# Attention and output projection of a hybrid trunk layer by seven block products (Strassen's scheme, Winograd's form) in place of eight

## The chip, the cores and the metric

One core of one Trainium2 chip runs the whole program. The metric is the device time of one execution in microseconds; the median of three runs of the kernel before is 1764.46 us (1763.48 to 1765.0).

## What is computed

One streaming step of one layer, for 1024 prompt tokens and 8 times 16 sample tokens (NT = 1152 tokens together), with D_MODEL 1024. The reference, cut to what matters here:

```python
def trunk_layer(...):
    h = rms_norm(x, norm_g) * (1 + scale) + shift
    q, k, v, z_att, z_ssd, xbc, dt_raw, gates = jnp.split(h @ w_in, IN_SPLITS, axis=-1)
    ...
    att_branch = (o_att.reshape(b, s, ATT_WIDTH) * jax.nn.silu(z_att)) @ w_att_proj   # 1024 x 1024
    ...
    y = rms_norm(y per group, ssd_norm_g)                                             # y = scan * silu(z_ssd)
    ssd_branch = y @ w_ssd_proj                                                       # 2048 x 1024
    merged = jax.nn.sigmoid(g_att) * att_branch + jax.nn.sigmoid(g_ssd) * ssd_branch
    out = x + gate * (merged @ w_out)                                                 # 1024 x 1024
```

All data are float32. The change concerns two of the three products above: the one with `w_att_proj` and the one with `w_out`.

## The kernel before

Activations lie channel-major: 128 channels on the partitions, 1152 tokens along the free axis. A projection of 1024 channels reads 8 such operand blocks and makes 8 output blocks.

**A product.** A float32 product is made of three float16 products: each operand is split into a high half (ScalarE casts it with a scale, L627 for weights, L1946 for activations) and a low half (VectorE: value times scale minus high half, L628 and L1948), and TensorE adds high·high, high·low and low·high (L709, L710, L712) into one PSUM tile. `dense` (from L694) makes an output tile of 128 channels by 384 tokens with 8 steps over the operand blocks (4 in the SSD projection), three matmuls each; three tiles make an output block. Tiles called d, g and s come from three PSUM pools of 3, 3 and 1 slots (an s slot has two banks). The first output block of the att and of the output projection (`wide`) and the last one of a product (`last`) make their three tiles side by side, step by step.

**The tail of the program**, with which the change deals. The att projection runs first (`att_dense`, 8 jobs of one output block). Its operands are loaded from DRAM by `att_prep` (SyncE, L1961) and split by `split` (L1943 to L1953); its result is multiplied into the gate block, which `gate_loads` fetched (SyncE, L1969; the evict is L1998, VectorE reading PSUM). Next come four groups of the SSD projection (`ssd_dense(g)`, 4 jobs with two output blocks each, tiles of 12 matmuls): VectorE multiplies a tile with its gate (L2007, reads PSUM) and adds it to the att result (L2008, reads SBUF only). In group 3 each output block is then complete, and `split` makes it an operand of the output projection. Last is `out_dense`, 8 output blocks: VectorE adds gate times tile to x (L2070; the sample columns by L2074 and L2076), and SyncE stores the block (L2081 for the last block, tile by tile, L2083 for the others). Weights of 128×1024 float32 come from DRAM ahead of their use and are split by `w_split`; ScalarE also sums the squares of every weight and operand (`level`, L619). `verdict` (L2047 to L2060) compares these sums with bounds and writes `again`; at the end of the program every engine reads `again` (L3822) and would otherwise run a general kernel, which does not happen here.

**What sets the order.** The program is written as generators that emit work in the order of the dense products, with helper generators beside them (`urgent`, `pause`). A list scheduler, class `Order`, then fixes one order of instructions for each engine from a table of costs. Each engine runs its own list in order. Semaphores between the engines see to the data, so that an instruction that waits holds up all that stands behind it on its engine. GpSimd (Pool) has a mask multiplication of the SSD scan (L1816), small steps of the group norm, and the DMA issues of the stores of gates (L1659) and of y (L1892); it does nothing from the att projection's second half on.

Of the kernel before, what the change touches and what calls it, by code (L numbers as in the profile page):

```python
# [16 lines left out]
P = 128  # L17
# [47 lines left out]
X_MEAN = (0.25, 2.0 ** 19)  # L65

# [353 lines left out]
def trunk_kernel(ctx: ExitStack, tc: tile.TileContext, h, again):  # L420
# [42 lines left out]
    NPART, NOPER = 121, 48  # L463
    sums = fix(NPART + 2 + NOPER)
# [34 lines left out]
    L_TAIL = arena.set_layout(Z0, [("T", 15, NT)])  # L499
    L_SM = arena.set_layout(Z0 + 15 * NT, [("e", 2, 384)])  # L500
# [14 lines left out]
    def alloc(lay, tag, cols):  # L515
        if lay is L_H or lay is L_W or lay is L_W3 or lay is L_Q or lay is L_V:
# [84 lines left out]
    def job(*raw):  # L601
        jobs.append([len(parts) + i for i in range(len(raw))])
        parts.extend(raw)
# [9 lines left out]
    meant = {"w": 0, "x": NPART + 2}  # L613
# [15 lines left out]

    def w_split(i, keep=lambda x: x):  # L630

        n = len(jobs[i])
# [44 lines left out]
    def w_done(i):  # L677
        for x in wsplit.pop(i)[:2]:
            x.free()
# [1255 lines left out]
    gates = []  # L1935

# [16 lines left out]

    att_ops, out_ops = [], []
    ssd_ops = [[] for _ in range(NG)]

    def att_prep():
        yield from ready(lambda: ssd_all[NPAIR])
        for u in range(NU):
            t = yield from walloc(L_TAIL, "T", NT)  # L1960
            dma(t.ap, att_d[u])  # L1961
            yield from pause(3000)
            urgent.append(split(t, att_ops, SA))

    def gate_loads():
        yield from ready(lambda: len(att_ops) >= NU - 1)
        for i in range(16):
            t = yield from walloc(L_TAIL, "T", NT)
            dma(t.ap, gate_d[i])  # L1969
            gates.append(t)  # L1970
            yield from pause(5000 if i < 2 else 10500)

    def ssd_prep(g):
        yield from ready(lambda: len(ssd_ops[g - 1]) == PPG if g else len(att_ops) == NU)
# [16 lines left out]
    def att_dense():  # L1991
        for c in range(8):
            def ev(o, g, tok, ps, c=c):
                while len(gates) <= c:
# [5 lines left out]
            yield from dense(att_ops, ev, last=c == 7, wide=c == 0, other=True)  # L2000

    def ssd_dense(g):
        for cp in range(4):
            def ev(o, g_, tok, ps, cp=cp):
# [42 lines left out]
    def verdict():  # L2047
        w, n = NPART + 2, NPART + 2 + NOPER
        assert meant == {"w": NPART, "x": n}
        nc.scalar.activation(sums[:, NPART:w], par["qk_g"], AF.Square, scale=4.0)  # L2050
        good = alloc(L_TAIL, "T", NT).ap
        ps = pg(NOPER)
        nc.tensor.matmul(ps, ones, sums[:, w:n], start=True, stop=True)
        for a, b, x, (least, most) in ((0, w, sums[:, :w], W_MEAN), (w, n, ps, (P * X_MEAN[0], X_MEAN[1]))):
            nc.vector.tensor_scalar(good[:, a:b], x, least, None, ALU.is_ge)
            nc.vector.scalar_tensor_tensor(good[:, a:b], sums[:, a:b], most, good[:, a:b], ALU.is_le, ALU.mult)
        nc.vector.tensor_reduce(good[:, n:n + 1], good[:, :n], mybir.AxisListType.X, ALU.min)
# [4 lines left out]
    def out_dense():  # L2062
        for c in range(8):
            x = yield from walloc(L_TAIL, "T", NT)
            dma(x.ap, h["xT"][c])

            def ev(o, g, tok, ps, c=c, x=x):
                n = G3 if g < 2 else NP - 2 * G3
                a = g * G3
                nc.vector.scalar_tensor_tensor(x.ap[:, a:a + n], ps[:, :n], m3[:, 16 + c, 0:1], x.ap[:, a:a + n], ALU.mult, ALU.add)  # L2070
                if g == 2:
                    t = alloc(L_SM, "e", P)
                    t3 = t.ap.rearrange("p (b s) -> p b s", s=NS)
                    nc.vector.tensor_tensor(t3, ps[:, n:].rearrange("p (b s) -> p b s", s=NS),  # L2074
                                            m3[:, 16 + c, 1:].unsqueeze(2).to_broadcast([P, NB, NS]), ALU.mult)
                    nc.vector.tensor_tensor(x.ap[:, NP:], x.ap[:, NP:], t.ap, ALU.add)  # L2076
                    t.free()
                if c == 7:
                    if g == 2:
                        verdict()  # L2080
                    dma(h["out_y"][c][:, tok], x.ap[:, tok])  # L2081
                elif g == 2:
                    dma(h["out_y"][c], x.ap)  # L2083
                    x.free()

            yield from dense(out_ops, ev, wide=c == 0, order=(2, 0, 1) if c == 7 else (0, 1, 2))
# [1880 lines left out]
```

## Time and profile before

The profiled execution took 1765.52 us, of which 1763.6 us are the span that the profile covers. The engines in that span:

| engine | busy us | share of the span |
|---|---|---|
| TensorE matmul (PE) | 1738.2 | 99% |
| TensorE weight load (PEld) | 1092.9 | 62% |
| VectorE (DVE) | 1230.0 | 70% |
| ScalarE (ACT) | 957.8 | 54% |
| GpSimd (POOL) | 347.3 | 20% |

The tail by the stretches of the trace (start of the first to start of the next product's first matmul):

| stretch | from us | to us |
|---|---|---|
| att projection | 1376.8 | 1476.0 |
| SSD projection, 4 groups | 1476.0 | 1663.2 |
| output projection | 1663.2 | 1757.3 |
| after the last matmul | 1757.3 | 1763.6 |

How to read it: an engine's busy time is the time in which an instruction of it runs, register, branch and DMA-issuing instructions left out. A row of the timeline gives an instruction's start, its duration, engine, line, operation, what it writes and reads, and in brackets the idle time before it with what ended it. Since successive matmuls overlap, the price of one is the distance from start to start, and not its duration.

### The profile page before, as it was taken

The numbers are of one execution on the slowest core, as the hardware profiler recorded it, in microseconds if no ns is written. First come the engines' busy times: TensorE is split into PE (matmuls) and PEld (weight loads), VectorE is DVE, ScalarE is ACT, GpSimd is POOL, SyncE is SP. The second block draws the span as 40 slices with busy tenths as digits, with TensorE's granted clock in tenths as the row PEclk, the third lists the DMA queues.
The fourth block names the chain that finished last, engine by engine and source line by source line (L and its number), as shares of the span: only waits on it lengthen the run. The fifth ranks groups of instructions, "written<-read, shape, count | busy, mean of one in ns | idle before, by whom it ended". The sixth has DMA issues, their size and how long they took to land.

```text
span 1763.6 us, 34941 instructions
## 1 busy us (share of the span) xinstructions
PE 1738.2 (99%) x13821; PEld 1092.9 (62%) x13821; DVE 1230.0 (70%) x2327; ACT 957.8 (54%) x1903; POOL 347.3 (20%) x624
## 2 busy tenths in 40 slices
PE   7999999999999999999999999999999999999998
PEld 3556556555556566666666666666666556666665
DVE  6458677877776967787878677777775526876732
ACT  8766555556465565656764656456552616342510
POOL 0233323323133011321312131112222100000000
PEclk9999999999999999999999999999999999999999
DMA  9248878988887584533554445435577734311321
GB/s 381 74 125 206 196 213 198 206 211 195 204 232 165 148 230 131 174 114 124 174 158 114 107 132 181 140 117 133 165 227 271 270 103 156 102 49 50 128 104 56
DMA packets 266565, 284.87 MB, mean 162 GB/s; under 512 B 199628, under 2 KB 200664, under 8 KB 266392
## 3 DMA queue, kind: packets, MB, share of 16 engines
q1 hardware_dynamic: 257432, 253.90, 51.9%
q0 software_dynamic: 8960, 28.65, 4.3%
q8 instruction: 110, 1.80, 0.4%
q14 instruction: 63, 0.52, 0.1%
HBM read 192.70 MB, written 43.66 MB: 134 GB/s over the span
## 4 chain that ended last, share of the span: by engine, by line
PE 87%; DVE 5%; ACT 4%; DMA 2%; issue 1%; POOL 1%; SPq 0%; DVEq 0%; POOLq 0%; ACTq 0%
PE d L709 19%; PE d L710 18%; PE d L712 18%; PE d L762 5%; PE d L764 5%; PE d L763 5%; PE g L1368 2%; PE s L1855 2%; PE g L1827 2%; PE g L1875 1%; PE s L1415 1%; PE g L1415 1%; PE g L712 1%; PE g L710 1%; PE g L709 1%
## 5 line engine op out<-in xcount | busy, mean ns | idle before, releaser
L709 PE MATMUL d<-arena 128*128 128x384 f16 x2172 | 709.6, 327 | 1.4 <-ACT arena L1543 1.4
L710 PE MATMUL d<-arena 128*128 128x384 f16 x2172 | 708.7, 326 | 0.0
L712 PE MATMUL d<-arena 128*128 128x384 f16 x2172 | 708.6, 326 | 0.0
L709 PEld LDWEIGHTS <-arena 128*128 128x128 f16 x2280 | 223.5, 98 | 147.8 <-issue 10.5
L712 PEld LDWEIGHTS <-arena 128*128 128x128 f16 x2280 | 223.2, 98 | 147.8 <-issue 0.5
L710 PEld LDWEIGHTS <-arena 128*128 128x128 f16 x2280 | 223.3, 98 | 138.0 <-issue 2.0
L619 ACT ACTIVATE arena<-arena 128x1024 bf16<-128x1024 f32 (+3 forms) x169 | 181.5, 1074 | 145.0 <-DMA arena<-in_wall_dram 82.4
L627 ACT ACTIVATE arena<-arena 128x1024 f16<-128x1024 f32 (+1 forms) x117 | 122.4, 1046 | 124.5 <-PE d L710 112.6
L762 PE MATMUL d<-arena 128*128 128x384 f16 (+1 forms) x568 | 186.8, 329 | 0.0
L764 PE MATMUL d<-arena 128*128 128x384 f16 (+1 forms) x568 | 186.1, 328 | 0.0
L763 PE MATMUL d<-arena 128*128 128x384 f16 (+1 forms) x568 | 186.1, 328 | 0.0
L628 DVE SCALAR_TENSOR_TENSOR arena<-arena 128x1024 f16<-128x1024 f32 (+1 forms) x117 | 145.3, 1246 | 42.3 <-ACT arena L627 41.7
L1308 ACT ACTIVATE arena<-arena 128x640 f32<-128x640 f32 (+4 forms) x144 | 100.8, 701 | 62.6 <-DVE arena L1311 62.1
L1566 DVE SCALAR_TENSOR_TENSOR arena<-arena 128x1176 f32<-128x1176 f32 x72 | 107.2, 1489 | 2.3 <-issue 0.9
L1754 ACT ACTIVATE arena<-arena 128x128 f32<-128x128 f32 x288 | 89.9, 390 | 28.0 <-DMA arena<-acs_d 26.3
L762 PEld LDWEIGHTS <-arena 128*128 128x128 f16 x576 | 56.3, 98 | 50.7 <-issue 17.5
L1344 DVE SCALAR_TENSOR_TENSOR arena<-arena 128x640 f16<-128x640 f32 (+4 forms) x128 | 86.9, 711 | 0.0
L1236 POOL TENSOR_SCALAR arena<-arena 128x16 f32<-128x16 f32 (+1 forms) x24 | 10.0, 415 | 356.3 <-DVE arena L1209 356.1
L764 PEld LDWEIGHTS <-arena 128*128 128x128 f16 x576 | 56.4, 98 | 38.4 <-issue 0.2
L1203 ACT ACTIVATE arena<-d 128x256 f32<-128x256 f32 x71 | 26.8, 378 | 96.1 <-PE d L764 96.1
L763 PEld LDWEIGHTS <-arena 128*128 128x128 f16 x576 | 56.4, 98 | 32.8
L1311 DVE CUSTOM_DVE_ANT_0 arena<-s,arena 128x320 f32<-128x320 f32 (+4 forms) x128 | 60.2, 502 | 19.4 <-PE s L1473 9.4
(242 smaller groups left out, 2596.4 us busy)
## 6 DMA issues: line engine op xcount, KB each, us to landing
arena<-in_wall_dram SPq DMA_DIRECT2D x85, 512.0 KB
arena<-acs_d SPq DMA_DIRECT2D x32, 576.0 KB
arena<-in_kc_dram SPq DMA_DIRECT2D x64, 256.0 KB
arena<-in_vc_dram SPq DMA_DIRECT2D x64, 256.0 KB
arena<-in_wada_dram SPq DMA_DIRECT2D x24, 512.0 KB
arena<-in_xT_dram SPq DMA_DIRECT2D x16, 576.0 KB
gate_d<-arena POOLq DMA_DIRECT2D x48, 192.0 KB, 4.0
arena<-eacs_d SPq DMA_DIRECT2D x32, 288.0 KB
```

Source lines behind the costliest of these rows:

```text
L619: keep(nc.scalar.activation(junk[:, :n], x, AF.Square, scale=scale * n ** -0.5, accum_out=sums[:, c:c + 1]))
L627: keep(nc.scalar.activation(hi, x, AF.Copy, scale=scale))
L628: keep(nc.vector.scalar_tensor_tensor(lo, x, scale, hi, ALU.mult, ALU.subtract))
L709: nc.tensor.matmul(ps, hi.r[:, wc], kh.r[:, tok], start=k == 0, stop=False)
L710: nc.tensor.matmul(ps, hi.r[:, wc], kl.r[:, tok], start=False, stop=False)
L712: nc.tensor.matmul(ps, lo.r[:, wc], kh.r[:, tok], start=False, stop=k == nk - 1)
L762: nc.tensor.matmul(ps, kh.r[:, tok], wh, start=k == 0, stop=False)
L763: nc.tensor.matmul(ps, kh.r[:, tok], wl, start=False, stop=False)
L764: nc.tensor.matmul(ps, kl.r[:, tok], wh, start=False, stop=k == KT - 1)
L1308: nc.scalar.activation(p, p, AF.Exp, bias=sm_[:, 4 + e:5 + e], scale=-1.0, accum_out=sm_[:, 6 + e:7 + e])
L1566: nc.vector.scalar_tensor_tensor(yc, r.ap[:, j:j + n], w4[:, i, j:j + 1], yc, ALU.mult, ALU.add)
L1754: nc.scalar.activation(me[e].ap[:, cs], me[e].ap[:, cs], AF.Relu, scale=-1.0, bias=a4[:, c, hds[e]:hds[e] + 1])
```

## The change

The att and the output projection are done in pairs. Two output blocks c and c+1, the even and odd operand blocks, and the first and second 576 tokens make a 2×2 product of blocks; where eight block products stood, seven are made (q0 to q6), each with 4 steps over pairs of operand blocks. `quad_dense` makes a product as two tiles of 128×288, in the order 0, 1, 5, 6, 4, 3, 2, with the banks taken from the pools s, g and d in turn. What the scheme needs beside the products:

- `quad_split`: four sums of 128×512 weights on Pool for each pair of output blocks; halves of 1024, 1024, 1024 and 512 columns (before: twice 1024).
- `pieces` in place of `split`: for each pair of operand blocks four sums of 128×576 on Pool; halves of 576, 1152, 1152 and 1152 columns (before: twice 1152), and four sums of squares of 576 columns.
- joins: ScalarE copies q0 out of PSUM; six products are joined with a running sum by seven joins of two VectorE additions 128×288 each (one operand in SBUF, one in PSUM; q4 is added into two sums).
- the evicts take 128×576 from SBUF instead of 128×384 from PSUM (att: L2191; out: L2281, and L2284 and L2285 for the samples); the output is stored in 16 parts of 128×576 (L2286).

With these go two more slots of 128×1152 in the tail, loads of gates held back until blocks are used up (`gone`), and a longer `verdict` (emitted with the last pair's product 4). New line numbers: matmuls L776 to L778, joins L790, Pool sums L659 to L662 and L2130 to L2133, halves L635/L636 and L2114/L2116, SSD evicts L2202/L2203, loads of att operands L2151.

```diff
+    def quad_split(i):
...
+        halves(bufs[0].r, bufs[1].r, w[0].ap, SW)
+        nc.gpsimd.tensor_tensor(t[0], b[0], b[1], ALU.add)
+        nc.gpsimd.tensor_tensor(t[1], t[0], a[0], ALU.subtract)
+        nc.gpsimd.tensor_tensor(t[2], a[0], b[0], ALU.subtract)
+        nc.gpsimd.tensor_tensor(t[3], a[1], t[1], ALU.subtract)
...
+        halves(bufs[3].r, bufs[4].r, u[0].ap, SW)
+        halves(k4(bufs[2].r[:, :512]), k4(bufs[2].r[:, 512:]), b[1], SW)
+        halves(bufs[5].r, bufs[6].r, u[1].ap, SW)
...
-    for x in [h["wall"][i] for i in range(29, 85)] + [h["watt"][i] for i in range(8)] + [h["wssd"][i] for i in range(16)] \
-            + [h["wout"][i] for i in range(8)]:
-        job(x)
...
+    for i in range(0, 8, 2):
+        job(h["watt"][i], h["watt"][i + 1], quad=True)
...
+    def quad_dense(ops, evict, last=False):
...
+        def product(q, banks):
+            for k in range(4):
+                while len(ops) <= k:
+                    blocked[0] = "operand"
+                    yield None
+                wh, wl = w(q, k)
+                xh, xl = ops[k][q][:2]
+                for g, ps in enumerate(banks):
+                    c = slice(g * HC, (g + 1) * HC)
+                    nc.tensor.matmul(ps, wh, xh[:, c], start=k == 0, stop=False)
+                    nc.tensor.matmul(ps, wh, xl[:, c], start=False, stop=False)
+                    nc.tensor.matmul(ps, wl, xh[:, c], start=False, stop=k == 3)
+                    yield 3 * 122.0
...
+                nc.vector.tensor_tensor(y.ap[:, c], t.ap[:, c], ps, op)
...
+        b = bank(0)
+        yield from product(0, b)
+        s1 = yield from walloc(L_TAIL, "T", HT)
+        for g, ps in enumerate(b):
+            nc.scalar.activation(s1.ap[:, g * HC:(g + 1) * HC], ps, AF.Copy)
+        b = bank(1)
+        yield from product(1, b)
+        c = yield from joined(s1, b, ALU.add)
+        yield from evict(0, 0, c) or ()
+        b = bank(2)
+        yield from product(5, b)
+        u2 = yield from joined(s1, b, ALU.add)
...
+        b = bank(6)
+        yield from product(2, b)
+        c = yield from joined(u4, b, ALU.add)
+        u4.free()
+        yield from evict(0, 1, c) or ()
+        w_done(i)
...
+    def pieces(ta, tb, ops, scale):
...
+        got[0], = yield from halved(b11, HT)
+        got[1], got[2] = yield from halved(tb.ap[:, :NT], NT)
...
+        nc.gpsimd.tensor_tensor(t1, b12, b11, ALU.subtract)
+        nc.gpsimd.tensor_tensor(t2, b22, t1, ALU.subtract)
+        nc.gpsimd.tensor_tensor(t3, b22, b12, ALU.subtract)
+        nc.gpsimd.tensor_tensor(t4, t2, b21, ALU.subtract)
...
+        got[4], got[5] = yield from halved(u[0].ap[:, :NT], NT)
+        u[0].free()
+        got[6], got[3] = yield from halved(u[1].ap[:, :NT], NT)
...
     def att_dense():
-        for c in range(8):
-            def ev(o, g, tok, ps, c=c):
...
-                x = gates[c].ap[:, tok]
-                nc.vector.scalar_tensor_tensor(x, x, 1.0, ps, ALU.add, ALU.mult)
...
+                x = gates[c + o].ap[:, t * HT:(t + 1) * HT]
+                nc.vector.scalar_tensor_tensor(x, x, 1.0, y.ap, ALU.add, ALU.mult)
...
+            yield from quad_dense(att_ops, ev, last=c == 6)
+            gone[0] = c + 2
...
                 if g == NG - 1 and g_ == 2:
                     gates[8 + c].free()
-                    urgent.append(split(gates[c], out_ops, 0.5 * SM / (SA * SW)))
-
+                    if o:
+                        urgent.append(pieces(gates[c - 1], gates[c], out_ops, 0.5 * SM / (SA * SW)))
...
     def out_dense():
...
+                nc.vector.scalar_tensor_tensor(x.ap[:, a:a + n], y.ap[:, :n], m[:, 0:1], x.ap[:, a:a + n], ALU.mult, ALU.add)
+                if t:
+                    y3 = y.ap[:, n:].rearrange("p (b s) -> p b s", s=NS)
+                    nc.vector.tensor_tensor(y3, y3, m[:, 1:].unsqueeze(2).to_broadcast([P, NB, NS]), ALU.mult)
+                    nc.vector.tensor_tensor(x.ap[:, NP:], x.ap[:, NP:], y.ap[:, n:], ALU.add)
+                dma(h["out_y"][c + o][:, a:a + HT], x.ap[:, a:a + HT])
```

The change also moves instructions on the engines that feed TensorE. Names such as d_17612 are PSUM tiles of the pool d; `arena` is the SBUF.

**VectorE in the last SSD group, before** (L2007 and L2008 are the two evicts of a tile, L1948 a low half of an operand of the output projection, L628 one of a weight):

```order
L1948 SCALAR_TENSOR_TENSOR arena<-arena 128x1152
L2008 TENSOR_TENSOR arena<-arena 128x384
L2007 SCALAR_TENSOR_TENSOR arena<-arena,d_17415 128x384
L2008 TENSOR_TENSOR arena<-arena 128x384
L2007 SCALAR_TENSOR_TENSOR arena<-arena,d_17431 128x384
L2008 TENSOR_TENSOR arena<-arena 128x384
L628 SCALAR_TENSOR_TENSOR arena<-arena 128x1024
L2007 SCALAR_TENSOR_TENSOR arena<-arena,d_17446 128x384
L1948 SCALAR_TENSOR_TENSOR arena<-arena 128x1152
```

VectorE there after the change (L2202 and L2203 are the same evicts, L2116 a low half of an operand or of sums of operands, L636 one of a weight):

```order
L2202 SCALAR_TENSOR_TENSOR arena<-arena,d_17612 128x384
L2116 SCALAR_TENSOR_TENSOR arena<-arena 128x1152
L2203 TENSOR_TENSOR arena<-arena 128x384
L2202 SCALAR_TENSOR_TENSOR arena<-arena,d_17629 128x384
L2116 SCALAR_TENSOR_TENSOR arena<-arena 128x1152
L2203 TENSOR_TENSOR arena<-arena 128x384
L2202 SCALAR_TENSOR_TENSOR arena<-arena,d_17648 128x384
L2116 SCALAR_TENSOR_TENSOR arena<-arena 128x1152
L2203 TENSOR_TENSOR arena<-arena 128x384
L2202 SCALAR_TENSOR_TENSOR arena<-arena,d_17664 128x384
L2116 SCALAR_TENSOR_TENSOR arena<-arena 128x576
```

A low half stands between the two evicts of each tile, four in a row, where before there were one or two in four tiles.

**Pool in the last SSD group, after the change** (the sums of a pair of operands of the output projection and those of its first pair of weights):

```order
L2130 TENSOR_TENSOR arena<-arena 128x576
L2131 TENSOR_TENSOR arena<-arena 128x576
L2132 TENSOR_TENSOR arena<-arena 128x576
L2133 TENSOR_TENSOR arena<-arena 128x576
L659 TENSOR_TENSOR arena<-arena 128x512
L2130 TENSOR_TENSOR arena<-arena 128x576
L660 TENSOR_TENSOR arena<-arena 128x512
L661 TENSOR_TENSOR arena<-arena 128x512
L662 TENSOR_TENSOR arena<-arena 128x512
L2131 TENSOR_TENSOR arena<-arena 128x576
L2132 TENSOR_TENSOR arena<-arena 128x576
L2133 TENSOR_TENSOR arena<-arena 128x576
```

Before, Pool's list holds nothing at this place: its last stores of gates (L1659) stand directly ahead of the end of the program (L3822).

**VectorE at the end of the program, before** (the last tiles of the last output block, d_18289 and d_18316):

```order
L2057 TENSOR_REDUCE arena<-arena 128x1
L2060 TENSOR_SCALAR again<-g_18285 1x1
L2070 SCALAR_TENSOR_TENSOR arena<-d_18289,arena 128x384
L2070 SCALAR_TENSOR_TENSOR arena<-d_18316,arena 128x384
L3822 TENSOR_LOAD again
```

and after it (s_18812 are the two banks of the last product, g_18777 the 1×1 result of the verdict's matmul):

```order
L2264 TENSOR_REDUCE arena<-arena 128x1
L2281 SCALAR_TENSOR_TENSOR arena<-arena 128x576
L790 TENSOR_TENSOR arena<-arena,s_18812 128x288
L2267 TENSOR_SCALAR again<-g_18777 1x1
L790 TENSOR_TENSOR arena<-arena,s_18812 128x288
L2281 SCALAR_TENSOR_TENSOR arena<-arena 128x448
L2284 TENSOR_TENSOR arena<-arena 128x128
L2285 TENSOR_TENSOR arena<-arena 128x128
L4027 TENSOR_LOAD again
```

Behind the last matmul one evict stood on VectorE; now there stand the verdict's write and, behind the join, three more instructions.

More of the change, by code (lines that the diff above doesn't have):

```diff
@@ L65 @@
 X_MEAN = (0.25, 2.0 ** 19)
+H_MEAN = (0.25, 2.0 ** 14)
 class NoSlot(Exception):
@@ L1935, in trunk_kernel @@
     gates = []
+    gone = [0]
     def gates_dense():
@@ L1991, in att_dense, with ev @@
     def att_dense():
[L1992 to L1994 removed]
+        for c in range(0, 8, 2):
+            def ev(o, t, y, c=c):
+                while len(gates) <= c + o:
                     blocked[0] = "gates"
                     yield None
[L1997 to L2000 removed]
+                x = gates[c + o].ap[:, t * HT:(t + 1) * HT]
+                nc.vector.scalar_tensor_tensor(x, x, 1.0, y.ap, ALU.add, ALU.mult)
+                y.free()
+            yield from quad_dense(att_ops, ev, last=c == 6)
+            gone[0] = c + 2
     def ssd_dense(g):
@@ L2062, in out_dense, with ev @@
     def out_dense():
[L2063 to L2086, printed above, removed]
+        for c in range(0, 8, 2):
+            xs = []
+            for o in range(2):
+                x = yield from walloc(L_TAIL, "T", NT)
+                dma(x.ap, h["xT"][c + o])
+                xs.append(x)
+            def ev(o, t, y, c=c, xs=xs):
+                x, n = xs[o], HT if t == 0 else NP - HT
+                a = t * HT
+                m = m3[:, 16 + c + o, :]
+                nc.vector.scalar_tensor_tensor(x.ap[:, a:a + n], y.ap[:, :n], m[:, 0:1], x.ap[:, a:a + n], ALU.mult, ALU.add)
[4 more added lines that the diff above has]
+                dma(h["out_y"][c + o][:, a:a + HT], x.ap[:, a:a + HT])
+                y.free()
+                if c == 6 and (o, t) == (1, 1):
+                    verdict()
+            yield from quad_dense(out_ops, ev)
     def head_dense():
```

174 lines of the change are left out of this document (154 added, 20 removed).

## The prediction

> **What bounds the kernel now.** I read the page first: busy times, the clock and the chain that ended last.
>
> ```profile
> PE 1738.2 (99%) x13821; PEld 1092.9 (62%) x13821; DVE 1230.0 (70%) x2327; ACT 957.8 (54%) x1903; POOL 347.3 (20%) x624
> ...
> PEclk9999999999999999999999999999999999999999
> ...
> PE 87%; DVE 5%; ACT 4%; DMA 2%; issue 1%; POOL 1%; SPq 0%; DVEq 0%; POOLq 0%; ACTq 0%
> ```
>
> TensorE is busy 99% of the span at the full granted clock, and holds 87% of the chain. So the number of matmul columns is the time, as long as the others keep up. Whether they do is read where the change works, in the table by stretch (us, then busy time and count of PE, PEld, DVE, ACT, POOL, then clock, DMA share, GB/s): the att projection, the last SSD group, the output projection.
>
> ```profile
> 1376.80:1476.00 99.20, 99.20 (x627) 58.80 (x625) 39.36 (x53) 37.91 (x57) 3.97 (x10) 1.00 0.48 174
> 1619.40:1666.20 46.80, 46.80 (x290) 28.18 (x288) 35.98 (x58) 22.54 (x29) 0.00 (x0) 1.00 0.34 109
> 1663.20:1757.30 94.10, 94.10 (x581) 56.44 (x579) 32.02 (x61) 21.31 (x31) 0.00 (x0) 1.00 0.27 97
> ```
>
> In both projections that change, VectorE is busy for 40% and 34% of the time: room for more. In the last SSD group it is busy 36.0 of 46.8 us already: there is the narrow place. Pool is idle in all of these but for the start of the att projection.
>
> **The matmuls.** First and last of a stretch of 18 matmuls with 384 columns, and of 15 with 416 (start, duration):
>
> ```profile
> 1749.11 0.33 PE L709 MATMUL d<-arena 128*128 128x384 f16 x1
> ...
> 1751.87 0.33 PE L712 MATMUL d<-arena 128*128 128x384 f16 x1
> 544.77 0.34 PE L762 MATMUL d<-arena 128*128 128x416 f16 x1
> ...
> 547.24 0.34 PE L764 MATMUL d<-arena 128*128 128x416 f16 x1
> ```
>
> From start to start that is 2.76/17 = 0.1624 us at 384 columns and 2.47/14 = 0.1764 at 416. In proportion to the columns 288 take 0.1218 us; along the line through both, 0.1201. Before, each projection has 8 blocks × 3 tiles × 8 steps × 3 = 576 matmuls, 1152 in both: 187.1 us. After, 4 pairs × 7 products × 4 steps × 2 tiles × 3 = 672 each, 1344: 163.7 us (161.4 by the line). The gain is **−23.4 us**, bounds −22 (a row's rounding) and −25.7.
>
> What could hold that up is the weight load, which does not shrink:
>
> ```profile
> L709 PEld LDWEIGHTS <-arena 128*128 128x128 f16 x901 | 88.4, 98 | 59.6 <-issue 2.3
> ```
>
> A load takes 98 ns and runs beside the matmul before it; 122 ns still cover it, so I add nothing. On this the Trainium skill, "TensorE: Matmul & The Clock Gate", section "Back-to-back issue gap", speaks against the change: a stream of pairs of load and matmul is given as some 81 ns at 128 columns and 131 at 512. By an estimate between those figures 384 columns would take 114 ns and 288 take 102, and 1344 × 102 against 1152 × 114 would lose some 6 us. The trace differs, with 162.4 ns at 384 columns, and the rows decide.
>
> **The end.** Now one evict stands behind the last matmul:
>
> ```profile
> 1757.34 0.62 DVE L2070 SCALAR_TENSOR_TENSOR arena<-d,arena 128x384 f32<-128x384 f32 x1 [3.28 <-PE d L712]
> ```
>
> After, the order has join, write of `again` (which waits for a 1×1 matmul behind the last product), join, 448 columns, and two of 128. Durations by these rows:
>
> ```profile
> L2074 DVE TENSOR_TENSOR arena<-d,arena 128x128 f32<-128x128 f32 x7 | 2.0, 280 | 0.0
> L1909 DVE TENSOR_TENSOR arena<-arena,g 128x512 f32<-128x512 f32 x4 | 2.7, 680 | 1.2 <-PE g L1900 1.2
> ```
>
> That is 0.28 us at 128 columns and 0.68 at 512, so some 0.45 for a join, 0.61 for 448. The first join begins before the last matmuls end; 0.2 + 0.45 + 0.61 + 0.28 + 0.28 and half of a join make 2.0, against 0.62: +1.4, and +0.1 for a store of 576 columns in place of 384. **+1.5 us** (0.7 to 2.5).
>
> **Pool and VectorE hold each other up.** The change gives Pool 64 sums: 32 of 512 columns and 32 of 576. By size, from the rows of another Pool addition:
>
> ```profile
> L1240 POOL TENSOR_TENSOR arena<-arena 128x1024 f32<-128x1024 f32 x16 | 30.8, 1925 | 0.1
> L1240 POOL TENSOR_TENSOR arena<-arena 128x256 f32<-128x256 f32 x8 | 5.0, 627 | 0.2
> ```
>
> 1.06 us and 1.17 us, 71 us in all, on an engine that is idle there. They are not free for VectorE:
>
> ```profile
> 1323.93 1.22 DVE L628 SCALAR_TENSOR_TENSOR arena<-arena 128x1024 f16<-128x1024 f32 x1 [3.29 <-ACT arena L627]
> 1354.77 1.64 DVE L628 SCALAR_TENSOR_TENSOR arena<-arena 128x1024 f16<-128x1024 f32 x1
> 1354.56 2.31 POOL L1816 TENSOR_TENSOR rarena<-rarena,arena 128x256 fp32r<-128x256 f32 x2 [1.41 <-PE g L1900]
> 1376.35 0.20 POOL L590 TENSOR_TENSOR arena<-arena 128x9 f32<-128x9 f32 x1
> 1377.48 1.23 POOL L590 TENSOR_TENSOR arena<-arena 128x9 f32<-128x9 f32 x1
> 1377.30 1.36 DVE L1948 SCALAR_TENSOR_TENSOR arena<-arena 128x1152 f16<-128x1152 f32 x1 [0.84 <-ACT arena L1946]
> ```
>
> The same VectorE instruction took 1.22 us alone and 1.64 beside a Pool instruction that began 0.21 us before it; a Pool instruction took 0.20 alone and 1.23, when a VectorE one had begun 0.18 before it, and ended 0.05 after that one. Both sides read two operands from SBUF: one waits for the other. A Pool sum can thus cost VectorE up to its own 1.1 us.
>
> **The last SSD group.** VectorE's pace there, start to start, in before:
>
> ```profile
> 1641.02 1.22 DVE L628 SCALAR_TENSOR_TENSOR arena<-arena 128x1024 f16<-128x1024 f32 x1
> 1642.16 0.55 DVE L2007 SCALAR_TENSOR_TENSOR arena<-arena,d 128x384 f32<-128x384 f32 x1
> 1642.62 1.35 DVE L1948 SCALAR_TENSOR_TENSOR arena<-arena 128x1152 f16<-128x1152 f32 x1
> 1643.89 0.55 DVE L2008 TENSOR_TENSOR arena<-arena 128x384 f32<-128x384 f32 x1
> 1644.36 0.55 DVE L2007 SCALAR_TENSOR_TENSOR arena<-arena,d 128x384 f32<-128x384 f32 x1
> 1644.94 0.56 DVE L2008 TENSOR_TENSOR arena<-arena 128x384 f32<-128x384 f32 x1
> ```
>
> A half of 1024 columns takes 1.14, of 1152 1.27, a tile's two evicts 0.47 + 0.58 = 1.05. (0.60 and 0.69 for 512 and 576, by the columns.) A tile of 12 matmuls takes TensorE 1.949 us. In the order of after, the 14 tiles 8 to 21 of 24 have beside their evicts six halves of 1152, two of 576, four of 1024 and one of 512: 14.7 + 7.6 + 1.4 + 4.6 + 0.6 = 28.9 us on VectorE against 27.3 on TensorE, 1.6 late. With the same stretch come some 14 Pool sums. One delays VectorE by nothing in a gap, by 0.5 where an evict from PSUM stands next (which the lock doesn't hold), by 1.1 before one from SBUF. VectorE has few gaps here, so I take 0.7: 9.8. Three d tiles let VectorE fall behind by two tiles less its own evict, 2 × 1.949 − 0.75 = 3.1. The stall of TensorE is 1.6 + 9.8 − 3.1 = **+8 us** (0 to 14).
>
> **The start of the att projection.** Operands come late here already:
>
> ```profile
> 1376.82 0.33 PE L709 MATMUL g<-arena 128*128 128x384 f16 x1
> 1383.87 1.36 DVE L1948 SCALAR_TENSOR_TENSOR arena<-arena 128x1152 f16<-128x1152 f32 x1 [0.31 <-ACT arena L1946]
> 1370.37 0.34 SPq L1141 DMA_DIRECT2D arena<-ya  x1
> 1374.15 0.20 POOL L1142 TENSOR_SCALAR arena<-arena 128x9 f32<-128x9 f32 x1 [8.34 <-DMA arena<-ya]
> ```
>
> The last operand is split by 1385.2, 8.4 us after the first matmul, and `wide` covers it with 7/8 of 72 matmuls of 0.1624, 10.2 us. After, the order has 75 matmuls, 9.1 us, before the last step of product 5, which needs the fourth pair's sums. On Pool these stand behind gate stores and the norm's small steps that wait for `ya` until 1374.1; four of 1.17 with waits, then a cast and a half of some 1.3 each, give 1384 to 1387 where 1385.9 is needed. Three sums are also ahead of the SSD mask (L1816, done 1356.87; its matmul began 1359.23, quoted next), 3.4 us in a gap of 2.4.
>
> ```profile
> 1359.23 0.77 PE L1900 MATMUL g<-rarena 128*128 128x256 f32 x4
> ```
>
> Together **+3 us** (0 to 9).
>
> **Inside the products.** A pair takes TensorE 168 × 0.1218 = 20.5 us. VectorE has 14 joins (6.3), four evicts (some 3.0), weight halves (4.0): some 13 us, and with four sums at 1.1 under 18. It fits on average; banks of joins that wait behind a half cost something: **+1.75** over eight pairs (0 to 5). Output stores and loads of x move as many bytes as before, in a stretch whose DMA share is 0.27: nothing.
>
> **The sum**: −23.4 + 1.5 + 8 + 3 + 1.75 = −9.1 us. The profiled execution took 1765.52, its span 1763.6 and 1.9 around it; that gives 1756.4. It stood 1.1 above the median of the runs, 1764.46, so I predict **1755 us**.
>
> **Rivals.**
> - *Hidden.* Pool sums fall into gaps of VectorE and the operands arrive in time. For it: Pool's 71 us are spread over some 380 us of tail, and ScalarE's waits leave gaps in VectorE (row L1948 at 1377.30 waited 0.84 for ScalarE). Against it: 28.9 us in 27.3. It gives 1764.5 − 23.4 + 1.5 = 1742.6.
> - *Slower: the lock at full price.* Each critical Pool sum delays the low half or evict behind it by its whole length, and each low half delays the sum that the next half needs. 14 × 1.1 in the last group and two fourth pairs (att and out) with 4 sums of 1.17 that wait 1.25 each, 2.4 × 8 = 19, and 1.6, less 3.1 for the three d tiles and less 2 us in hand at each of the two starts: 29 us; −23.4 + 29 + 1.5 = +7: 1772. It decides from 22 us of such waits, where the gain is gone, some 20 sums at full price. Against it: a Pool sum waits for one VectorE instruction at most, and evicts from PSUM pass. The Trainium skill, "SBUF — State Buffer", section "SBUF: two separate sides", has the pair of ports as a lock held for the whole instruction; by that each collision pays in full, as the rows above bear out, but not how many collide.
> - *The change doesn't do what it says*: matmuls keep 0.1624 at 288 columns, held by the loads. 1344 × 0.1624 = 218.3, +31: 1797. Against it: 98 ns of a load, and 0.1764 against 0.1624 at 416 columns.
>
> **How the numbers follow.** A measurement of this kernel can tell about 0.2%, 3.5 us, from no change: faster is under 1761, slower over 1768. My forecast (1748 to 1761) has 0.52, hidden (1742 to 1748) 0.24, stalls that eat most of the gain (1761 to 1768) 0.09, the lock at full price 0.12, no shrinking 0.03. Faster 0.76, same 0.09, slower 0.15. The range 1742 to 1767 leaves out 0.15 above and a little of hidden below; the unknown terms at their bounds (0 to 28 us of stall) span 1740 to 1772, whose ends need all of them at once.
>
> **What would show it.** Matmuls at L776 with 0.122 us from start to start; if 0.14 or more, the first step is wrong. TensorE idle in the last SSD group, before d tiles that L2202 frees: 8 us; under 3 shows the sums in gaps, over 12 the full price. L2203, L636 and L2116 longer than 0.55, 1.22 and 1.35 beside L659 to L662 and L2130 to L2133. TensorE idle before g and d tiles of products 5 and 6 near the att projection's start: 3. From the last matmul to the end of the span 7.8 in place of 6.3. What would prove me wrong is idle time in a place that I don't name, above all between the att projection and the last group, where only weights are summed.

## The result, and the profile after

The kernel became slower: 1787.04 us median (1779.14 to 1790.71 in four runs) against 1763.97, ratio 1.0116, interval 1.0101 to 1.0132. The runs of the kernel before lie within 1.8 us, those of the changed one within 11.6. The profiled execution took 1786.96 us, with a span of 1785.2.

The page of the changed kernel, busy times, clock and chain:

```profile
PE 1726.9 (97%) x14013; PEld 1114.5 (62%) x14013; DVE 1336.7 (75%) x2461; ACT 995.0 (56%) x1983; POOL 456.8 (26%) x688
...
PEclk9999999999999999999999999999999999999999
...
PE 71%; DVE 10%; ACT 6%; DMA 5%; issue 5%; POOL 2%; SPq 0%; DVEq 0%; POOLq 0%; ACTq 0%
```

TensorE has 87% of the chain no longer, but 71%; VectorE, ScalarE, the transfers and issue gained. Pool is busy 109.5 us longer for the 64 sums, 1.71 us each, where 71 us, 1.11 each, were forecast.

The matmuls themselves did what they should. A stretch of 21 of the output projection:

```profile
1750.41 0.29 PE L776 MATMUL d<-arena 128*128 128x288 f16 x1
...
1752.86 0.29 PE L778 MATMUL d<-arena 128*128 128x288 f16 x1
```

That is 2.45/20 = 0.1225 us from start to start (1287 of the 1343 distances are of this kind and have a mean of 0.1225). 1344 × 0.1225 = 164.6 against 187.1: −22.5 us. All else goes the other way. The places where TensorE waited, from the timeline of PE; eight of the 20 rows from 1302 us on, where the first instruction of the change stands (before, this stretch has no wait). In brackets the wait and what ended it:

```profile
1368.88 1.37 PE L2043 MATMUL g<-rarena 128*128 128x256 f32 x4 [7.05 <-POOL rarena L1959]
1399.44 0.28 PE L777 MATMUL d<-arena 128*128 128x288 f16 x1 [1.07 <-DVE arena L2116]
1402.30 0.28 PE L776 MATMUL d<-arena 128*128 128x288 f16 x1 [2.09 <-DVE arena L790]
...
1653.24 0.32 PE L852 MATMUL d<-arena 128*128 128x384 f16 x1 [1.55 <-DVE arena L2202]
1663.46 0.32 PE L852 MATMUL d<-arena 128*128 128x384 f16 x1 [2.14 <-DVE arena L2202]
1679.49 0.32 PE L852 MATMUL d<-arena 128*128 128x384 f16 x1 [1.88 <-DVE arena L2202]
...
1710.14 0.28 PE L776 MATMUL g<-arena 128*128 128x288 f16 x1 [2.07 <-DVE arena L790]
1734.73 0.40 PE L776 MATMUL s<-arena 128*128 128x288 f16 x1 [3.12 <-DVE arena L790]
```

By stage, with the first matmul of each (1387.93, 1485.78, 1683.39 in the changed kernel; 1376.82, 1475.96, 1663.16 before) and the last (1776.92; 1756.97):

| stretch | changed by | of which fewer columns | waits and slow clock |
|---|---|---|---|
| up to the att projection | +11.1 | 0 | +11.1 |
| att projection | −1.3 | −11.25 | +9.95 |
| SSD projection | +10.4 | 0 | +10.4 |
| output projection | −0.3 | −11.25 | +10.95 |
| after the last matmul | +1.6 | 0 | +1.6 |
| sum | +21.5 | −22.5 | +44.0 |

The span grew by 21.6. Not all of the first row belongs to the change. Of the 11.1 us, 2.3 are there at 754 us, where both kernels still run the same instructions. TensorE waits there for an earlier mask, before and after:

```profile
746.99 0.80 PE L1900 MATMUL g<-rarena 128*128 128x256 f32 x2 [2.04 <-POOL rarena L1816]
```

```profile
747.90 0.80 PE L2043 MATMUL g<-rarena 128*128 128x256 f32 x2 [2.50 <-POOL rarena L1959]
```

Behind this wait the granted clock is 0.50 for 3.4 us before (747.0 to 750.4) and for 6.8 us after (747.25 to 754.07). With the sums on VectorE (an experiment below) the clock stays at 1.00 behind the same wait of 2.50. So the clock behind this wait differs between executions of the same instructions; between these last two it makes 3.0 us. The other 8.8 us arise at the wait of 7.05 us for the mask ahead of the att projection and just behind it. In the SSD projection the first three groups take the same time before and after; all of the 10.4 us lie in the last group.

The rows below show what a wait is made of; VectorE and Pool in the last SSD group, in one stretch of time:

```profile
1649.09 1.96 DVE L2116 SCALAR_TENSOR_TENSOR arena<-arena 128x1152 f16<-128x1152 f32 x1
1650.98 1.75 DVE L2203 TENSOR_TENSOR arena<-arena 128x384 f32<-128x384 f32 x1
1652.65 0.54 DVE L2202 SCALAR_TENSOR_TENSOR arena<-arena,d 128x384 f32<-128x384 f32 x1
1653.12 1.35 DVE L2116 SCALAR_TENSOR_TENSOR arena<-arena 128x576 f16<-128x576 f32 x1
1654.39 1.62 DVE L2203 TENSOR_TENSOR arena<-arena 128x384 f32<-128x384 f32 x1
```

```profile
1648.31 1.52 POOL L659 TENSOR_TENSOR arena<-arena 128x512 f32<-128x512 f32 x1 [3.49 <-DVE arena L2116]
1649.80 2.52 POOL L2130 TENSOR_TENSOR arena<-arena 128x576 f32<-128x576 f32 x1
1652.28 1.58 POOL L660 TENSOR_TENSOR arena<-arena 128x512 f32<-128x512 f32 x1
1653.82 1.78 POOL L661 TENSOR_TENSOR arena<-arena 128x512 f32<-128x512 f32 x1
```

The two engines take turns. The sum at 1649.80 waits for the low half that ends at 1651.05, then runs until 1652.32; the evict L2203, 0.55 us alone, is listed from 1650.98 to 1652.73: it waits for that sum. L2202, which reads PSUM, stays at 0.54. From 1649.09 to 1663.33 VectorE took 14.2 us for twelve instructions whose own pace adds up to some 8.0 to 8.4 (by 0.94 or 1.05 for a tile's two evicts), beside eight sums: 0.73 to 0.78 us a sum (forecast: 0.7).

Ahead of the att projection Pool is late. In its timeline the SSD mask L1959, for which TensorE waits 7.05 us, stands behind these:

```profile
1360.36 0.56 POOL L2035 DMA_DIRECT2D y_d<-arena  x1 [2.25 <-DVE arena L2031]
1360.94 1.52 POOL L662 TENSOR_TENSOR arena<-arena 128x512 f32<-128x512 f32 x1
1362.43 2.50 POOL L2130 TENSOR_TENSOR arena<-arena 128x576 f32<-128x576 f32 x1
1364.88 0.57 POOL L1802 DMA_DIRECT2D gate_d<-arena  x1
1365.48 1.80 POOL L2131 TENSOR_TENSOR arena<-arena 128x576 f32<-128x576 f32 x1
1367.24 2.16 POOL L1959 TENSOR_TENSOR rarena<-rarena,arena 128x256 fp32r<-128x256 f32 x2
```

The first of these rows is the store of y. Pool stood idle 2.25 us until VectorE's multiplication L2031 was done. L2031 began at 1358.70, and at 1350.11 in the first experiment below, where the sums are left out. So the mask is late for two reasons: VectorE reached L2031 8.6 us late, and from the store on Pool took 6.9 us to reach the mask. Seven more sums stand ahead of the store, from 1345.60 on.

And a wait costs more than its length. After the one at 1402.30:

```profile
1402.30 0.28 PE L776 MATMUL d<-arena 128*128 128x288 f16 x1 [2.09 <-DVE arena L790]
1402.43 0.28 PE L777 MATMUL d<-arena 128*128 128x288 f16 x1
...
1403.20 0.44 PE L778 MATMUL d<-arena 128*128 128x288 f16 x1
1403.44 0.44 PE L776 MATMUL d<-arena 128*128 128x288 f16 x1
```

The matmuls go from 0.12 to 0.24 us from start to start, half the clock, for some 3 us (after 1734.73 for 5.7). In windows of 2 us the granted clock is 0.50 there, though the page's row shows only nines, since each of its digits covers 45 us. From 1302 us on some 44 float16 matmuls ran so and lost some 5 us.

### The profile page after: what moved, and what is told of

It reads as the page before. It is cut to its first block, busy times and chain, and to the rows that moved or that the text cites. A ratio compares the mean times of both kernels' runs of the same rounds, so it can differ in the third digit from the quotient of the medians.

```text
span 1785.2 us, 35702 instructions
## 1 busy us (share of the span) xinstructions
PE 1726.9 (97%) x14013; PEld 1114.5 (62%) x14013; DVE 1336.7 (75%) x2461; ACT 995.0 (56%) x1983; POOL 456.8 (26%) x688
## 4 chain that ended last, share of the span: by engine, by line
PE 71%; DVE 10%; ACT 6%; DMA 5%; issue 5%; POOL 2%; SPq 0%; DVEq 0%; POOLq 0%; ACTq 0%
PE d L852 13%; PE d L853 12%; PE d L855 12%; PE d L905 5%; PE d L907 4%; PE d L906 4%; PE g L1511 2%; DVE arena L636 2%; PE s L1998 1%; DVE arena L2116 1%; PE g L1970 1%; DMA arena<-arena 1%; PE g L2018 1%; PE g L1558 1%; PE s L1558 1%
## 5 line engine op out<-in xcount | busy, mean ns | idle before, releaser
L852 PE MATMUL d<-arena 128*128 128x384 f16 x1860 | 608.8, 327 | 10.5 <-DVE arena L2202 9.0
L853 PE MATMUL d<-arena 128*128 128x384 f16 x1860 | 607.9, 327 | 0.0
L855 PE MATMUL d<-arena 128*128 128x384 f16 x1860 | 607.7, 327 | 0.0
L853 PEld LDWEIGHTS <-arena 128*128 128x128 f16 x1896 | 186.0, 98 | 124.4 <-issue 13.6
L855 PEld LDWEIGHTS <-arena 128*128 128x128 f16 x1896 | 185.9, 98 | 123.5 <-issue 1.3
L852 PEld LDWEIGHTS <-arena 128*128 128x128 f16 x1896 | 186.0, 98 | 122.2 <-issue 9.6
L627 ACT ACTIVATE arena<-arena 128x1024 bf16<-128x1024 f32 (+4 forms) x185 | 184.7, 998 | 110.3 <-DMA arena<-in_wall_dram 67.3
L636 DVE SCALAR_TENSOR_TENSOR arena<-arena 128x1024 f16<-128x1024 f32 (+2 forms) x133 | 173.9, 1312 | 45.7 <-ACT arena L635 45.4
L635 ACT ACTIVATE arena<-arena 128x1024 f16<-128x1024 f32 (+2 forms) x133 | 135.8, 1021 | 100.1 <-PE d L853 41.2
L905 PEld LDWEIGHTS <-arena 128*128 128x128 f16 x576 | 56.3, 98 | 50.7 <-issue 17.5
L907 PEld LDWEIGHTS <-arena 128*128 128x128 f16 x576 | 56.4, 98 | 38.4 <-issue 0.2
L906 PEld LDWEIGHTS <-arena 128*128 128x128 f16 x576 | 56.4, 98 | 32.8
```

The source lines that it names most:

```text
L627: keep(nc.scalar.activation(junk[:, :n], x, AF.Square, scale=scale * n ** -0.5, accum_out=sums[:, c:c + 1]))
L635: keep(nc.scalar.activation(hi, x, AF.Copy, scale=scale))
L636: keep(nc.vector.scalar_tensor_tensor(lo, x, scale, hi, ALU.mult, ALU.subtract))
L852: nc.tensor.matmul(ps, hi.r[:, wc], kh.r[:, tok], start=k == 0, stop=False)
L853: nc.tensor.matmul(ps, hi.r[:, wc], kl.r[:, tok], start=False, stop=False)
L855: nc.tensor.matmul(ps, lo.r[:, wc], kh.r[:, tok], start=False, stop=k == nk - 1)
```

## The experiments

**Theory**: Pool and VectorE exclude each other where both read two operands from SBUF; that lengthens both in an order that was made without it, and TensorE waits at each place where it has little in hand. **Rivals**: VectorE's own work is too much; or a sum on Pool is only slow, as a link between the halves.

**Sums not read.** This kernel leaves the sums out, so what it computes is not the layer.

```diff
-        nc.gpsimd.tensor_tensor(t1, b12, b11, ALU.subtract)
+        nc.gpsimd.tensor_tensor(t1[:, ::575], b12[:, ::575], b11[:, ::575], ALU.subtract); nc.gpsimd.memset(t1, 0.125)
...
```

> The 64 Pool sums are left out: each is a Pool addition of 2 or 4 elements and a fill of the same block, so Pool reads next to nothing; the order of the instructions on every engine is that of the changed kernel. Theory (Pool's and VectorE's reads of two SBUF operands exclude each other): the low halves and evicts are back at 1.27 and 0.47 us from start to start, the wait of 7 us for the mask ahead of the att projection and at least 8 of the 10 us in the last SSD group go, and with them the half clock: 1743 to 1755 us. Rival (VectorE's own load and its order are the bound, the lock is beside the point): most of the waits stay, 1775 or more. Rival (Pool is merely slow as a link between the halves): between the two, by as much as the fill is shorter than a sum.

Measured: 1746.60 us median, ratio to before 0.9892 (0.9875 to 0.9908), where the theory had it. In the traces TensorE, VectorE and ScalarE run the same instructions in the same order as in the changed kernel, and Pool differs in the sums alone. VectorE by groups between 1290 and 1790 us, the changed kernel first, then this one, then the same kinds before the change (busy us, mean ns of one, idle before):

```profile
L636 DVE SCALAR_TENSOR_TENSOR arena<-arena 128x1024 f16<-128x1024 f32 x45 | 66.0, 1470 | 13.0 <-ACT arena L635 13.0
L2203 DVE TENSOR_TENSOR arena<-arena 128x384 f32<-128x384 f32 x96 | 57.3, 610 | 1.1
L2116 DVE SCALAR_TENSOR_TENSOR arena<-arena 128x1152 f16<-128x1152 f32 x24 | 42.7, 1794 | 9.7 <-ACT arena L2114 9.7
```

```profile
L636 DVE SCALAR_TENSOR_TENSOR arena<-arena 128x1024 f16<-128x1024 f32 x45 | 55.0, 1229 | 7.2 <-ACT arena L635 7.2
L2203 DVE TENSOR_TENSOR arena<-arena 128x384 f32<-128x384 f32 x96 | 51.9, 554 | 1.1
L2116 DVE SCALAR_TENSOR_TENSOR arena<-arena 128x1152 f16<-128x1152 f32 x24 | 32.1, 1354 | 13.2 <-ACT arena L2114 13.2
```

```profile
L628 DVE SCALAR_TENSOR_TENSOR arena<-arena 128x1024 f16<-128x1024 f32 x37 | 45.6, 1232 | 12.0 <-ACT arena L627 11.9
L2008 DVE TENSOR_TENSOR arena<-arena 128x384 f32<-128x384 f32 x96 | 52.2, 554 | 1.7
L1948 DVE SCALAR_TENSOR_TENSOR arena<-arena 128x1152 f16<-128x1152 f32 x32 | 43.1, 1353 | 16.5 <-ACT arena L1946 16.3
```

The durations are those of before again, and from 1302 us on TensorE waits only three times, 1.2 us together. So the joins, the additional halves and VectorE's own 67 us of new work (1297.1 busy here against 1230.0) fit: the first rival falls. The 64 sums on Pool cost 40 us.

**Blocks filled twice.** The same with a second fill, so that Pool is busy nearly as long as in the changed kernel (449.0 us on the page against 456.8).

```diff
-...; nc.gpsimd.memset(t1, 0.125)
+...; nc.gpsimd.memset(t1, 0.125); nc.gpsimd.memset(t1, 0.125)
```

> As the kernel with fills in place of the sums, but each block filled twice, so that Pool is busy some 1.6 us per sum, about as long as a sum with its waits (1.7), and still reads next to nothing; the order is that of the changed kernel, and the sums are left out. Theory (the lock on VectorE's instructions is the loss): within 5 us of the single fill, 1745 to 1752 us. Rival (Pool's length as a link, and the mask behind the sums on Pool): most of the 40 us come back, 1770 or more; a split shows the share of each.

Measured: 1761.49 us median (1759.01 to 1763.14). Pool's length alone brings 15 of the 40 us back; the other 25, by difference, are the collisions. The theory's number (within 5 us) was missed: Pool is also late as a link, first of all for the mask:

```profile
1360.07 0.64 PE L2043 MATMUL g<-rarena 128*128 128x256 f32 x2 [1.99 <-POOL rarena L1959]
1361.75 0.80 PE L2043 MATMUL g<-rarena 128*128 128x256 f32 x2 [1.05 <-POOL rarena L1959]
```

**Sums on VectorE.**

```diff
-        nc.gpsimd.tensor_tensor(t1, b12, b11, ALU.subtract)
+        nc.vector.tensor_tensor(t1, b12, b11, ALU.subtract)
...
```

> The 64 sums on VectorE in place of Pool: no lock, but some 64 times 0.6 to 0.7 = 42 us more on VectorE, 14 to 24 of the sums in the last SSD group, where it has no time left: 9 to 14 us there. Theory (lock): a sum on Pool costs VectorE about what it costs on VectorE itself, so the time is within 10 us of the changed kernel, 1777 to 1795. Rival (Pool's length as a link of the chain is the loss): VectorE's shorter sums help, below 1770.

Measured: 1750.71 us median (1749.99 to 1757.81), ratio to before 0.9932 (0.9908 to 0.9955). This computes all and **beats both kernels**, by 14 us (before: 1765.16 in these runs) and by 36. Its page, and one of its groups of sums:

```profile
PE 1715.8 (98%) x14013; PEld 1111.4 (64%) x14013; DVE 1335.7 (76%) x2525; ACT 993.6 (57%) x1983; POOL 349.4 (20%) x624
```

```profile
L2130 DVE TENSOR_TENSOR arena<-arena 128x576 f32<-128x576 f32 x8 | 6.0, 752 | 4.0 <-DMA arena<-att_d 4.0
```

VectorE is busy 1335.7 us with the 64 sums on it, and 1336.7 with the sums on Pool: the collisions took as much of VectorE's time as the sums themselves would have. I had expected from this that the two kernels would take about the same time; they don't. VectorE's time is the same, but a sum of 576 columns takes 0.75 us and not 1.9 (mean of L2130 on Pool), the order was made with VectorE's sums in it, and Pool is free for the mask, for which TensorE no longer waits at the att projection. What each of these is worth wasn't separated.

**All sums on VectorE, and 64 more on Pool.** Additions of the same sizes on the same blocks, into a buffer that nobody reads (one more slot of the tail).

```diff
+        nc.gpsimd.tensor_tensor(z1, b12, b11, ALU.subtract)
+        nc.gpsimd.tensor_tensor(z2, b22, b11, ALU.subtract)
+        nc.gpsimd.tensor_tensor(z1, b22, b12, ALU.subtract)
+        nc.gpsimd.tensor_tensor(z2, b12, b21, ALU.subtract)
...
         nc.vector.tensor_tensor(t1, b12, b11, ALU.subtract)
...
```

> The kernel with all sums on VectorE, and beside them 64 additions of the same size on Pool, on the same blocks, whose results nobody reads: the lock without a sum as a link on Pool. Pool's occupation, with the mask behind it, is in both this and the kernel with two fills, which cost 15 us over one fill. Theory (lock on VectorE's instructions is the larger part): 64 times 0.6 us more on VectorE, 20 to 30 us over the kernel with the sums on VectorE alone, 1770 to 1780. Rival (a sum as a late link is what costs): 1752 to 1762.

Measured: 1804.87 us median, 54 us over the sums on VectorE alone.

```profile
PE 1731.1 (96%) x14013; PEld 1115.9 (62%) x14013; DVE 1390.8 (77%) x2525; ACT 994.6 (55%) x1983; POOL 465.1 (26%) x688
```

VectorE is busy 55.1 us longer, 0.86 us for each addition on Pool, though not one result of Pool is used. For VectorE's time that is the lock by itself, and more than either theory gave; a likely reason, not tested, is that more of VectorE's instructions read two SBUF operands here, so that there is more to collide with. The kernel's 54 us are not the lock alone. TensorE waits 5.54 us for the mask behind Pool's additions again, and VectorE waits three times, 7.8 us together, for Pool itself.

**One projection at a time.** The other one as before the change.

```diff
-    for i in range(0, 8, 2):
-        job(h["watt"][i], h["watt"][i + 1], quad=True)
+    for i in range(8):
+        job(h["watt"][i])
...
```

> Only the output projection by seven products, the att projection as before. By the changed kernel's stages (last SSD group +10, output projection 0, end +1.7) this stands at 1776 us if the stages are independent. If the waits of the last group came only from an order already upset by the late start, it stands near 1755 (half of the gain, 11 us, and the end).

> Only the att projection by seven products, the output projection as before. By the changed kernel's stages (start +11, att projection -1) this stands at 1774 us if the stages are independent; the last SSD group then has no Pool sums and must be as long as before. If the mask's wait goes, 1765.

Measured: only the output projection 1779.45 us median (ratio 1.0079, 1.0062 to 1.0096), only the att projection 1770.82 (1.0035, 1.0020 to 1.0049). The medians stand 14.3 and 5.7 us above before (1765.16 in these runs), 20 together, against 23 for both at once: the two nearly add up, and neither pays for itself. (With the output projection alone TensorE also waits 2.71 us at 1390.62, which neither kernel does.) The last group's waits are there without any change ahead of it, and the mask's wait is there with the att projection alone. From the two kernels in this order:

```profile
1661.19 0.32 PE L852 MATMUL d<-arena 128*128 128x384 f16 x1 [2.51 <-DVE arena L2196]
1728.63 0.28 PE L776 MATMUL s<-arena 128*128 128x288 f16 x1 [3.10 <-DVE arena L790]
```

```profile
1365.00 1.36 PE L2043 MATMUL g<-rarena 128*128 128x256 f32 x4 [6.63 <-POOL rarena L1959]
```

**A new plan.** Two kernels with the change's instructions and another table for the scheduler.

```diff
-        t = 250 + 180.0 * m if x.name in self.slow else 200 + 1.75 * m
+        t = 250 + 180.0 * m if x.name in self.slow else 1750.0 if m in (512, 576) else 200 + 1.75 * m
```

> The changed kernel planned anew with a sum's mean length under collisions, 1.75 us instead of 1.10 and 1.21, and no lock in the plan. If late sums in the order are the loss, most of it returns: 1750 to 1765 us. If VectorE's lengthened instructions are, little changes: 1775 to 1790.

```diff
...
+            if u["two"]:
+                o = "Pool" if e == "DVE" else "DVE"
+                t = max(t, lock[o])
+                lock[e] = t + busy
...
```

> The changed kernel with the sums on Pool, planned anew: the scheduler's table gets 1.28 and 1.41 us for a sum (the traces' times alone), and from the first sum on it lets no two-SBUF instruction of VectorE and of Pool run at the same time. If the loss is that the fixed order was made without the lock, the new one brings back most of it: 1745 to 1765 us. If the waits are inherent, because sums on Pool take VectorE's time and come late in any order, it stays above 1775.

Measured: 1777.10 us median with the longer sums, 1773.82 with the lock in the plan; 10 and 13 us better than the changed kernel, and still slower than before (1.0045, 1.0028 to 1.0062 for the lock). The first lies where VectorE's lengthened instructions were held to be the loss, the second between the two answers: of the 40 us that the sums cost, a new order with the lock in it brings back a third. With the lock in the plan the mask's wait is gone, but the kernel still has 19 us of waits and some 57 matmuls at half clock, and VectorE is busy 1344.6 us. Why a plan that knows the lock remains 23 us behind the sums on VectorE, with VectorE as busy, wasn't separated further and stays open.

**Only the weights' sums on Pool.**

```diff
-        nc.gpsimd.tensor_tensor(t1, b12, b11, ALU.subtract)
+        nc.vector.tensor_tensor(t1, b12, b11, ALU.subtract)
...
```

> The 32 sums of operands on VectorE, the 32 of weights on Pool as in the changed kernel. Weights are summed some 20 us ahead of their use, operands just in time. Theory (what counts is a sum on Pool as a late link of a chain that TensorE waits for): close to all sums on VectorE, 1748 to 1756 us. Rival (every sum on Pool costs alike by the lock): half way, 1765 to 1772.

Measured: 1763.85 us median (1759.04 to 1768.34), no difference from before (0.9992, 0.9978 to 1.0006). Of the 36 us between all sums on VectorE and all on Pool, the weights' half of the sums has 13. The rival ("every sum on Pool costs alike by the lock", 1765 to 1772) is nearer than the theory's number, and both missed. VectorE is busy 1328.3 us here, 7.4 less than with all sums on it, and yet the kernel is 13 us slower: its time doesn't follow from VectorE's busy time alone. From 1302 us on TensorE waits 15.7 us here, against 6.3 with all sums on VectorE; the two longest, 2.37 and 1.49, are for joins.

**Banks that turn on.** Behind the best kernel: neighbouring products of two pairs don't share the s slot.

```diff
-        def bank(n):
+        def bank(n, first=qturn[0]):
+            n += first
...
```

> The sums on VectorE, and the banks turn on from pair to pair: before, the last product of a pair and the first of the next both take the one s slot, so that TensorE waits for a join or a copy between them; now no two neighbours take the same pool. If such waits (1.3 us each twice in the kernel with the sums on VectorE) are still worth something: 1746 to 1750 us. If the order hides them already: 1749 to 1753, no difference.

Measured: 1755.03 us median (1752.70 to 1756.13), above both expectations, 4 us over the sums on VectorE with the banks as they were, and no better in any run than its three fastest. The intervals of the two overlap (0.9924 to 0.9957 against 0.9908 to 0.9955), so no gain is shown, and no loss either. The waits for the copy L805 became 0.81 and 1.02 us in place of 1.34 and 1.32, and others came (1.69 for a d tile at 1659.94).

## Why the prediction was wrong

**The matmuls** were right: 0.1225 us at 288 columns (forecast 0.1218), −22.5 us (−23.4). The weight loads do not hold the matmuls up, and the rival that columns don't shrink the time fell.

**The end** was right: +1.6 (forecast +1.5).

**The last SSD group** was right in mechanism and nearly in size: +10.4 (forecast +8, 0 to 14), 0.73 to 0.78 us per sum (0.7).

**The start of the att projection** is the step that failed first: "+3 us (0 to 9)". Measured were 8.8 us before it begins (11.1 less the 2.3 that have nothing to do with the change), and 4.9 us of waits in its first four rows, up to 1416, behind that. I had seen three sums ahead of the mask and priced them at 1.17 each, "3.4 us in a gap of 2.4". Ten stand ahead of it from 1345.60 on. The last three took 1.5 to 2.5 us, since they collide with VectorE, and they began late because the store ahead of them waited for VectorE's L2031, which the same collisions had made 8.6 us late. That a delayed VectorE holds up Pool in turn was in no term.

**Inside the products**: "It fits on average", +1.75 us (0 to 5). Measured were 7.5 us of waits in the output projection alone, and 2.2 in the att projection behind its start. The average was right (VectorE is busy 64.1 of 93.5 us in the output projection); but the order is fixed, and where a chain of sum, cast, low half and product is late by a few us, TensorE has nothing else to do.

**The clock** stood in no term. Of the seven waits of 1.5 us or more in the changed kernel from 1302 us on, three were followed by half clock; some 5 us were lost so on float16 matmuls. That TensorE runs "at the full granted clock" was read from the page, whose digits hide a stretch of 3.4 us; the trace of the kernel before has 0.50 from 747.0 to 750.4, behind the wait of 2.04 us.

In all, 14.25 us of delays were forecast (8, 3, 1.75 and 1.5), and the table has 44.0: 2.3 from ahead of the change, 8.8 at the mask, 9.95 and 10.95 in the two projections, 10.4 in the last SSD group and 1.6 at the end. So the lock was seen, quoted with its rows, and rightly priced at one place, the last SSD group; at the start and inside the products it was priced far too low. The rival that comes nearest is "the lock at full price", which I gave 0.12 and 1772 us. Its price of 1.1 us a sum is not what the last group shows (0.73 to 0.78), and the result lies 15 us beyond it. The mask's wait (7.05 us) and the half clock (some 5), which its sum doesn't have, would make up most of that, though no run separates them from the rest. Its objection, "a Pool sum waits for one VectorE instruction at most, and evicts from PSUM pass", holds in the rows, but does not help: with 28.9 us of work in 27.3, one instruction at a time is all VectorE has. That 64 sums times 0.7, 45 us, is close to the 44.0 is no rule: the weights' half of the sums cost 13 us. The Trainium skill, "SBUF — State Buffer", section "SBUF: two separate sides", speaks of the loser as fully blocked for the whole instruction; the rows at 1649 show just that.

## What to carry to other kernels

Work given to an idle Pool is not free when it reads two SBUF operands beside a busy VectorE: here 64 sums on Pool took as much of VectorE's time (0.62 us each) as the same sums on VectorE, and one of 576 columns took 2.5 times as long (1.9 us against 0.75). Count such instructions against VectorE first, then compare with simply putting them there; here that turned a loss of 23 us into a gain of 14. And where TensorE is the bound and the order is fixed, price a delayed feeder at every place where TensorE has little in hand, and not by the average of a stage.

## What the runs showed of the hardware

- VectorE and Pool, where both read two SBUF operands, alternate instruction by instruction: the same evict took 0.55 us alone and 1.75 beside a sum; a sum of 576 columns took 1.41 us without a wait and up to 2.52 with one. An evict that reads PSUM stayed at 0.54 beside the sums, and beside fills on Pool a low half of 1152 columns took 1.354 us, as before the change (1.353).
- A Pool addition of 576 float32 columns takes 1.41 us and one of 512 some 1.28, where rows of 256 and 1024 columns gave 1.17 and 1.06 by interpolation; a fill of 576 takes 0.58. On VectorE the addition takes 0.75.
- TensorE went to half clock, 0.24 us for 288 columns, after waits far shorter than I had thought worth a term, and not by length alone: in the changed kernel after 7.05, 2.09 (with 1.66 us of waits in the 8 us before) and 3.12, but not after 2.14; with only the weights' sums on Pool, after a single one of 1.49. At 747 us, where all kernels run the same instructions, a wait of 2.04 (before) was followed by 3.4 us of it, one of 2.50 by 6.8 us in the changed kernel and by none with the sums on VectorE. In most cases it lasted some 3.3 us (14 matmuls), in some twice that. The Trainium skill, "TensorE: Matmul & The Clock Gate", in the part on the HAM clock gate, gives an idle window of some 3.4 us as what brings the slow clock; the waits here were mostly shorter, so the rows decide.
